# The weight parts of a two-layer encoder kernel begin a few bytes off a 64-byte multiple, at another place in each stage

## The chip, the cores and the metric

The kernel is one program on one core of a Trainium2 chip. The metric is the device time of one execution in microseconds. Before the change it is 1512.05 us, the median of two runs (1512.05 and 1512.06).

The engines are named as the profile names them: PE is TensorE's matmul stream and PEld its weight loads, DVE is VectorE, ACT is ScalarE, POOL is GpSimd, SP is the engine that issues most transfers. A matmul of this kernel loads a 128 x 128 weight (the *loaded* operand) and then streams up to 512 columns of another tile through it (the *streamed* operand).

## The reference

The reference is a two-layer trunk over a sequence of 512 positions with 1,024 features, with a memory of 256 positions, all in float32:

```python
for layer in range(DEPTH):
    xn = rms_norm(x, mix_norm[layer])
    if layer % 2 == 0:
        mixed = fox_diff_mixer(xn, ...)      # forgetting + differential attention
    else:
        mixed = mlstm_mixer(xn, ...)         # chunkwise mLSTM
    x = x + mixed
    x = x + memory_cross_attention(rms_norm(x, ...), rms_norm(mem, ...), wq, wkv, wo)
    x = x + conv_ffn(rms_norm(x, ...), w_up, conv_w, conv_b, w_down)
return rms_norm(x, final_norm)
```

Each layer thus has three stages: a mixer, a cross-attention over the memory and a gated FFN with a depthwise convolution (hidden width 2 x 2816). Nearly all arithmetic is in products of activations with weights.

## The kernel before, in words

**Split products.** A float32 product is formed from parts. Each weight block arrives by DMA in a tile `raw` (128 x 1024 floats). ScalarE writes its rounded high part to a tile `wh` (`split`, L262, or L1159 in the FFN), VectorE subtracts and writes the rest to a tile `wl` (`sub`, L259). Both have the type fp32r. Activations are kept as two parts as well, `xh` and `xl`. `mm3` (L268 to L270) then issues three matmuls for one 128 x 128 block: wh with xh, wh with xl, wl with xh, all three into one PSUM bank. The weight part is the loaded operand there, the activation is streamed. In `p_proj_tok` (L329 to L331) it is the other way round: the activations are loaded and the weight parts are streamed; this makes the values of the attentions and of the mLSTM. In `p_gate` (L542, L543) the weight of a few gate columns, 40 in the first mixer and 100 in the second, is loaded from a `wh` tile in which eight such blocks lie one behind the other.

**The tiles.** `raw`, `wh` and `wl` come from one pool with three buffers each. Every tile of this size in the program begins at a multiple of 64 bytes within its partition (small paddings, `pad`, see to that for some). So every 128-column weight block, 512 bytes, begins on such a multiple too. I call a multiple of 64 a *line* below. Of the larger tiles only the second buffer of `hs`, the rows that the convolution reads, begins 32 bytes off one; the convolution's taps (L1254) read `hs` from element 0, 1 or 2 on, and its second half begins 514 elements in.

**Stages and order.** A planner (`Plan`) sets the order for mixers and cross-attentions, a list scheduler (`Sched`) for the FFNs, both in Python with their own cost figures while the program is written; each engine then works its list in order. Parts of the next cross-attention's memory projections are made within the mixer.

**The FFN.** The up projection of a pair of 128-column blocks is done in one of two ways: plainly with 512-column matmuls, or, for nine of 22 pairs a layer (`SEVEN`), by seven products of half size with 256-column matmuls (`seven`). Of these seven, four load from `wh` and `wl` tiles (X first, th into `s`, X second, th into `acc`, of 12 matmuls each); the others load from tiles of their own, `s2`, `s4` and `a22`. `th` and `tl` are prepared activations. Between the products lie `fill` steps, pieces of the down projection with 512-column matmuls (rows `w<-ah,wh`). The memory projections of the cross-attentions (rows `acc<-mem,wh` of 256 columns) and the last projections of the program (`acc<-ah,wh` of 256 columns) are the other 256-column work on `wh`.

Of the kernel before, what the change touches and what calls it, by code (L numbers as in the profile page):

```python
# [9 lines left out]
F32 = mybir.dt.float32  # L10
F32R = mybir.dt.float32r
# [5 lines left out]
P = 128  # L17
# [34 lines left out]
class Item:  # L52
    def __init__(self, fn, dur, deps, prio, take, free, chain, pre, after, order, load, st):
        self.fn, self.dur, self.deps, self.prio, self.st = fn, dur, list(deps), prio, st
        self.take, self.free, self.chain, self.pre, self.after = take, free, chain, pre, after
        self.order, self.load = [o for o in order if o is not None], load
        self.ready = None


class Plan:  # L60
# [11 lines left out]
    def add(self, fn, dur=0.0, deps=(), prio=None, take=(), free=(), chain=(), pre=(), after=0.0, order=(), load=(), st=None):  # L72
        it = Item(fn, dur, [d for d in deps if d is not None], len(self.items) if prio is None else prio, take, free, chain, pre, after, order, load, st)
        it.n = len(self.items)
        self.items.append(it)
        return it
# [138 lines left out]
        self.now, self.idle = now, idle  # L215


class Builder:
    def __init__(self, tc, t):
        self.tc, self.nc, self.t = tc, tc.nc, t  # L220
# [26 lines left out]


    def weight_tiles(self):
        return [self.til(self.wp, tag, (P, 1024), dtype, bufs=3) for tag, dtype in (("raw", F32), ("wh", F32R), ("wl", F32R))]  # L250

    def weight(self, src, cols=1024):
        raw, hi, lo = self.weight_tiles()
# [264 lines left out]
    def gate_weights(self, src, m, parts):  # L518

        nc = self.nc  # L520
        raw = self.til(self.sp, "gw", (P, 8, m), bufs=1)
        nc.scalar.dma_start(raw[:], src)
        both = self.til(self.wp, "wh", (P, 1024), F32R, bufs=3)[:, : 8 * parts[-1][2]].rearrange("p (a b) -> p a b", a=8)
        nc.vector.memset(both.bitcast(F32), 0.0)
        for a, hi, lo, n in [(p[0], p[1], p[2] - p[3], p[3]) for p in parts]:
            h = both[:, :, hi : hi + n]
            nc.vector.tensor_copy(h, raw[:, :, a : a + n])
            self.sub(both[:, :, lo : lo + n], raw[:, :, a : a + n], h)
        return both
# [589 lines left out]
    def ffn_steps(self, layer, mp):  # L1119
# [3 lines left out]
        nc, t = self.nc, self.t  # L1123
# [23 lines left out]
            return add("SP", 0.0017 * cols, fn, (), at, [(tag, st)], (), 2.0)  # L1147

        def parts(st):
            st["wh"], st["wl"] = (self.til(self.wp, n, (P, 1024), F32R, bufs=3) for n in ("wh", "wl"))  # L1150

        def weight(src, cols, at, tag="raw"):

            st = {}
            l = load(st, tag, src, cols, at - 9.0)

            def hi():
                parts(st)
                nc.scalar.copy(st["wh"][:, :cols], st[tag][:, :cols])  # L1159

            h = add("ACT", act(cols), hi, [l], at - 3.0, [("h", st)])
            lo = add("DVE", tt(cols), lambda: self.sub(st["wl"][:, :cols], st[tag][:, :cols], st["wh"][:, :cols]), [h], at - 2.0, (), [(tag, st)])
            return st, lo
# [137 lines left out]
        def seven(p, fill):  # L1301
# [24 lines left out]
            def sum4(out, a, b):  # L1326
                if not sums.get("t"):
                    sums["t"] = self.til(mp, "sum", (P, 1536), bufs=1)
                tt_(out=out(), in0=a(), in1=b(), op=ALU.add)

            w3 = split(f3, 1024, [l2], at, lambda: parts(f3), [("h", f3)], lambda: r2["raw"][:])
            b1 = add("DVE", tt(512), lambda: sum4(S1, A21, A22), [l1], at - 6.0, [("sum", sums)])
            b2 = add("DVE", tt(512), lambda: sum4(S2, S1, A11), [b1, l2], at - 5.5)
            b3 = add("DVE", tt(512), lambda: sum4(S3, A21, A11), [b1, l2], at - 5.0)
            w2 = split(s2, 512, [b2], at, lambda: small(s2, "s2"), [("s2", s2)], S2)
            b4 = add("DVE", tt(512), lambda: sum4(S4, S2, A12), [w2], at - 1.5)
            w1 = split(f1, 1024, [b3], at + 1.0, lambda: parts(f1), [("h", f1)], lambda: sums["t"][:, :1024])
            w22 = split(a22, 512, [l1], at + 4.0, lambda: small(a22, "a22"), [("a22", a22)], A22)
            w4 = split(s4, 512, [b4], at + 5.0, lambda: small(s4, "s4"), [("s4", s4)], S4)
# [95 lines left out]
        if layer == 0:  # L1435
            for m in range(8):
                e = down(4, m, 2)
                a = add("ACT", 1.43, lambda m=m: self.xprep(m, "mix", 1, state), [e], clock[0] + 3.0)
# [261 lines left out]
    def run(self):  # L1700
        tc = self.tc
        M = bass.MemoryType.PSUM
        with (
            tc.tile_pool(name="cp", bufs=1) as self.cp,
            tc.tile_pool(name="xp", bufs=1) as self.xp,
            tc.tile_pool(name="sp", bufs=1) as self.sp,
            tc.tile_pool(name="wp", bufs=1) as self.wp,
            tc.tile_pool(name="acc", bufs=1, space=M) as self.acc,
            tc.tile_pool(name="aux", bufs=1, space=M) as self.aux,
        ):  # L1710
            self.constants()
            self.pad(self.cp, 32)
            self.pad(self.sp, 64)
            for layer in range(2):
                with tc.tile_pool(name=f"mem{layer}", bufs=1, reuse_waits="tile") as self.memp:
                    (self.mix0, self.mix1)[layer]()
                    self.xattn(layer)
                self.ffn(layer)


# [86 lines left out]
```

## Time and profile before

| | |
|---|---|
| median of the runs | 1512.05 us |
| the profiled execution | 1512.78 us |
| its span, first to last instruction | 1511.0 us |
| granted TensorE clock, mean over the span | 0.998 |
| PE busy, matmuls | 1500.0 us, 8026 |
| PEld busy, loads | 1281.7 us, 8026 |
| DVE busy | 1160.1 us |
| ACT busy | 774.8 us |
| POOL busy | 44.0 us |
| read from HBM | 143.04 MB |

The profiled execution is one run of the program; the span leaves out what lies before its first and behind its last instruction. A row of the groups gives line, engine, operation, out<-in tiles, shape and count, then busy time and mean of one in ns, then the engine's idle time in front. Matmuls overlap in the records: a mean of 390 ns doesn't say how far apart they start. The timeline gives each instruction's start and duration in us. The view of one line gives min/median/max in ns.

The stages follow each other like this: first mixer to about 262 us, cross-attention to 405, FFN to 768; second mixer to about 1015, cross-attention to 1166, FFN to the end.

### The profile page before, as it was taken

To read this page: it belongs to the slowest core of one execution; us is meant where nothing else is said; L and a number is where in the kernel's file an instruction comes from. 1 tells how busy PE (TensorE), PEld (TensorE's weight loads), DVE (VectorE), ACT (ScalarE), POOL (GpSimd) and SP (SyncE) were. 2 spreads that over 40 slices of the span, in tenths; PEclk is the share of its full clock that TensorE was granted. 3 is DMA by queue.
4 is the path that set the end of the run, shared out by engine and by line. 5 is a ranking of instruction groups with operands and counts; after the bars stand their busy time and mean duration, and the time that the engine had idled before them with its cause. 6 is when DMAs were issued, how large, how long until landed. Compare 5 with 4: busy or idle time off the path is not lost.

```text
span 1511.0 us, 21313 instructions
## 1 busy us (share of the span) xinstructions
PE 1500.0 (99%) x8026; PEld 1281.7 (85%) x8026; DVE 1160.1 (77%) x2155; ACT 774.8 (51%) x1282; POOL 44.0 (3%) x118
## 2 busy tenths in 40 slices
PE   9999999999999999999999999999999999999998
PEld 8888888888888888988888778888888888888887
DVE  7889885766699788897678857666557988889864
ACT  6768564444465444454446634444445554444444
POOL 2000120000000000000001100000000000000000
PEclk9999999999999999999999999999999999999999
DMA  5222233323223333232222222332323332333322
GB/s 179 84 71 84 84 103 108 112 96 100 95 101 100 97 108 109 84 112 88 81 90 84 80 89 93 99 101 99 111 84 109 108 94 95 98 103 106 102 60 77
DMA packets 47480, 146.52 MB, mean 97 GB/s; under 512 B 5649, under 2 KB 5649, under 8 KB 47377
## 3 DMA queue, kind: packets, MB, share of 16 engines
q1 hardware_dynamic: 46368, 144.04, 29.4%
q8 instruction: 63, 1.03, 0.3%
q10 hardware_dynamic: 1008, 1.12, 0.2%
q14 instruction: 41, 0.33, 0.1%
HBM read 143.04 MB, written 2.10 MB: 96 GB/s over the span
## 4 chain that ended last, share of the span: by engine, by line
PE 92%; DVE 3%; ACT 2%; issue 1%; DMA 1%; POOL 0%; SPq 0%; DVEq 0%; POOLq 0%; ACTq 0%
PE acc L268 19%; PE acc L269 19%; PE acc L270 19%; PE w L269 5%; PE w L268 5%; PE w L270 5%; PE acc L330 2%; PE acc L331 2%; PE acc L329 2%; PE s L268 2%; PE s L269 2%; PE s L270 2%; PE w L1595 1%; PE w L681 1%; PE s L395 1%
## 5 line engine op out<-in xcount | busy, mean ns | idle before, releaser
L268 PE MATMUL acc<-xh,wh 128*128 128x512 f32 (+1 forms) x944 | 356.9, 378 | 0.0
L270 PE MATMUL acc<-xh,wl 128*128 128x512 f32 (+1 forms) x944 | 352.8, 374 | 0.0
L269 PE MATMUL acc<-xl,wh 128*128 128x512 f32 (+1 forms) x944 | 352.6, 374 | 0.0
L259 DVE TENSOR_TENSOR wl<-raw,wh 128x1024 fp32r<-128x1024 f32 (+2 forms) x215 | 258.0, 1200 | 51.9 <-ACT wh L262 38.1
L262 ACT CAST wh<-raw 128x1024 fp32r<-128x1024 f32 (+2 forms) x137 | 140.9, 1030 | 168.5 <-PE acc L269 99.6
L270 PEld LDWEIGHTS acc<-xh,wl 128*128 128x128 f32 x944 | 177.5, 188 | 31.7
L268 PEld LDWEIGHTS acc<-xh,wh 128*128 128x128 f32 x944 | 177.6, 188 | 30.4
L269 PEld LDWEIGHTS acc<-xl,wh 128*128 128x128 f32 x944 | 177.7, 188 | 30.3
L1254 DVE SCALAR_TENSOR_TENSOR c<-hs,vec,c 128x512 f32<-128x512 f32 x176 | 128.4, 746 | 7.4 <-ACT c L1247 6.8
L269 PE MATMUL w<-al,wh 128*128 128x512 f32 x304 | 118.5, 390 | 0.0
L268 PE MATMUL w<-ah,wh 128*128 128x512 f32 x304 | 118.5, 390 | 0.0
L270 PE MATMUL w<-ah,wl 128*128 128x512 f32 x304 | 118.3, 389 | 0.0
L1159 ACT CAST wh<-raw 128x1024 fp32r<-128x1024 f32 (+1 forms) x60 | 61.3, 1022 | 77.8 <-PE acc L269 49.3
L1247 ACT ACTIVATE c<-hs,vec 128x512 f32<-128x512 f32 x88 | 70.0, 812 | 40.2 <-DVE hs L1393 23.5
L495 DVE TENSOR_TENSOR x<-w,x 128x512 f32<-128x512 f32 x72 | 49.5, 687 | 31.9 <-PE w L270 31.6
L270 PEld LDWEIGHTS w<-ah,wl 128*128 128x128 f32 x304 | 57.1, 188 | 12.0
L268 PEld LDWEIGHTS w<-ah,wh 128*128 128x128 f32 x304 | 57.1, 188 | 10.9
L269 PEld LDWEIGHTS w<-al,wh 128*128 128x128 f32 x304 | 57.1, 188 | 10.7
L1159 ACT CAST wh<-dr 128x512 fp32r<-128x512 f32 x64 | 39.7, 620 | 47.9 <-issue 17.4
L1268 ACT CAST ah<-c 128x512 fp32r<-128x512 f32 x44 | 27.3, 620 | 68.9 <-DVE c L1264 68.9
L330 PE MATMUL acc<-wl,xh 128*128 128x256 f32 (+1 forms) x192 | 61.9, 323 | 0.2 <-DVE wl L259 0.2
L329 PE MATMUL acc<-wh,xh 128*128 128x256 f32 (+1 forms) x192 | 61.7, 326 | 0.0
(373 smaller groups left out, 3323.4 us busy)
## 6 DMA issues: line engine op xcount, KB each, us to landing
raw<-in_up_dram SPq DMA_DIRECT2D x88, 512.0 KB, 3.3
dr<-in_down_dram SPq DMA_DIRECT2D x64, 256.0 KB, 2.6
raw<-in_xk_dram SPq DMA_DIRECT2D x16, 512.0 KB, 3.3
raw<-in_wo_dram SPq DMA_DIRECT2D x16, 512.0 KB, 3.2
raw<-in_xq_dram SPq DMA_DIRECT2D x16, 512.0 KB, 3.3
raw<-in_xv_dram SPq DMA_DIRECT2D x16, 512.0 KB, 3.3
raw<-in_xo_dram SPq DMA_DIRECT2D x16, 512.0 KB, 3.3
raw<-in_down_dram SPq DMA_DIRECT2D x16, 384.0 KB, 3.0
```

What stands on the lines that cost most here:

```text
L259: self.nc.vector.tensor_tensor(out=lo, in0=v, in1=hi.bitcast(F32), op=ALU.subtract)
L262: self.nc.scalar.copy(hi, v)
L268: mm(out, wh, xh, start=first, stop=False, skip_group_check=parts)
L269: mm(out, wh, xl, start=False, stop=False, skip_group_check=parts)
L270: mm(out, wl, xh, start=False, stop=last, skip_group_check=parts)
L329: mm(ps, xh[k][:, ts], wh[:, ws], start=(k == 0), stop=False)
L330: mm(ps, xh[k][:, ts], wl[:, ws], start=False, stop=False)
L331: mm(ps, xl[k][:, ts], wh[:, ws], start=False, stop=(k == 7))
L495: self.nc.vector.tensor_tensor(out=self.x[m][:], in0=ps[:], in1=self.x[m][:], op=ALU.add)
L1159: nc.scalar.copy(st["wh"][:, :cols], st[tag][:, :cols])
L1247: nc.scalar.activation(st["c_"][:, j, :], hs()[:, j, 2:514], AF.Identity, scale=self.col("cw", (layer * 3 + 2) * 44 + blk), bias=self.col( ...
L1254: nc.vector.scalar_tensor_tensor(out=c, in0=hs()[:, j, n : n + 512], scalar=w, in1=c, op0=ALU.mult, op1=ALU.add)
```

## The change

The tiles `wh` and `wl` get 1,088 columns in place of 1,024, and the parts are written to and read from columns `place` to `place + 1024`. `place` is set for each stage:

| | mixer | cross-attention | FFN |
|---|---|---|---|
| layer 0 | 2 (8 bytes) | 3 (12 bytes) | 1 (4 bytes) |
| layer 1 | 4 (16 bytes) | 60 (240, 16 below 256) | 63 (252, 4 below 256) |

`raw`, `dr` and the activations stay where they were in their tiles, and so do `s2`, `s4` and `a22`. The gates' weights, which share the tile `wh`, move too. The six tiles grow by 256 bytes each; to make room, the area for descriptors of dynamic DMAs at the start of the memory goes from 16,384 to 1,024 bytes. All other tiles thereby lie 13,824 to 15,360 bytes lower, by whole multiples of 512 outside the pool of `raw`, `wh` and `wl` and by multiples of 256 within it.

```diff
+PLACES = ((2, 3, 1), (4, 60, 63))
...
     def weight_tiles(self):
-        return [self.til(self.wp, tag, (P, 1024), dtype, bufs=3) for tag, dtype in (("raw", F32), ("wh", F32R), ("wl", F32R))]
+        return [self.til(self.wp, "raw", (P, 1024), bufs=3), self.part_tile("wh"), self.part_tile("wl")]
+
+    def part_tile(self, tag):
+
+        return self.til(self.wp, tag, (P, 1088), F32R, bufs=3)[:, self.place : self.place + 1024]
...
         nc.scalar.dma_start(raw[:], src)
-        both = self.til(self.wp, "wh", (P, 1024), F32R, bufs=3)[:, : 8 * parts[-1][2]].rearrange("p (a b) -> p a b", a=8)
+        both = self.part_tile("wh")[:, : 8 * parts[-1][2]].rearrange("p (a b) -> p a b", a=8)
...
         def parts(st):
-            st["wh"], st["wl"] = (self.til(self.wp, n, (P, 1024), F32R, bufs=3) for n in ("wh", "wl"))
+            st["wh"], st["wl"] = (self.part_tile(n) for n in ("wh", "wl"))
...
                 with tc.tile_pool(name=f"mem{layer}", bufs=1, reuse_waits="tile") as self.memp:
+                    self.place = PLACES[layer][0]
                     (self.mix0, self.mix1)[layer]()
+                    self.place = PLACES[layer][1]
                     self.xattn(layer)
+                self.place = PLACES[layer][2]
                 self.ffn(layer)
...
-    nc = _bacc.Bacc("TRN2", target_bir_lowering=False, num_devices=1)
+    nc = _bacc.Bacc("TRN2", target_bir_lowering=False, num_devices=1, dynamic_dma_scratch_size=1024)
```

## The prediction

> **What bounds the kernel now.** I read the page first: the busy times and the chain that ended last.
>
> ```profile
> span 1511.0 us, 21313 instructions
> PE 1500.0 (99%) x8026; PEld 1281.7 (85%) x8026; DVE 1160.1 (77%) x2155; ACT 774.8 (51%) x1282; POOL 44.0 (3%) x118
> ...
> PE 92%; DVE 3%; ACT 2%; issue 1%; DMA 1%; POOL 0%; SPq 0%; DVEq 0%; POOLq 0%; ACTq 0%
> ```
>
> TensorE is busy 99% of the span, and 92% of the chain is its own instructions one behind the other. Then the waits: first TensorE's view, whose weight row is the last below, then ScalarE's, whose longest wait stands in the second fence.
>
> ```profile
> PE acc L330 <- DVE wl L259: 0.2, 1, 0.2
> ```
>
> ```profile
> ACT wh L262 <- PE acc L269: 99.6, 40, 4.4
> ```
>
> TensorE waited for a weight's low part once, for 0.2 us. ScalarE, which makes the high part, waited 99.6 us for TensorE to release a buffer. So the parts are ready early, and neither engine that makes them sets the end. What counts is the time from one matmul's start to the next. Busy means (390 ns and so on) overlap and don't show it; the timeline of TensorE does. First, how many matmuls read a changed tile (by line and form; each L268 row has twins of the same count in L269 and L270):
>
> ```profile
> L268 PE MATMUL acc<-xh,wh 128*128 128x512 f32 x800 | 316.4, 395 | 0.0
> L268 PE MATMUL w<-ah,wh 128*128 128x512 f32 x304 | 118.5, 390 | 0.0
> L268 PE MATMUL acc<-mixed,wh 128*128 128x512 f32 x104 | 40.9, 393 | 0.1
> L268 PE MATMUL acc<-xh,wh 128*128 128x256 f32 x144 | 40.5, 281 | 0.0
> L268 PE MATMUL acc<-mem,wh 128*128 128x256 f32 x128 | 36.6, 286 | 0.0
> L329 PE MATMUL acc<-wh,xh 128*128 128x256 f32 x128 | 36.5, 293 | 0.0
> L268 PE MATMUL acc<-mem,wh 128*128 128x512 f32 x64 | 24.9, 389 | 0.0
> L268 PE MATMUL acc<-th,wh 128*128 128x256 f32 x72 | 20.2, 280 | 0.0
> L268 PE MATMUL s<-th,wh 128*128 128x256 f32 x72 | 19.9, 276 | 0.0
> L268 PE MATMUL acc<-mh,wh 128*128 128x512 f32 x48 | 19.0, 395 | 0.0
> L268 PE MATMUL acc<-ah,wh 128*128 128x256 f32 x36 | 10.3, 285 | 0.0
> ```
>
> With the changed tile as the loaded weight there are (800+304+104+64+48) x 3 = 3,960 matmuls of 512 columns, and (144+128+72+72+36) x 3 = 1,356 of 256. In L329 to L331 the weight is the streamed operand instead: the row of 128 above, times 3, and as many again of 512 columns.
>
> Now the pace, in the timeline of one block of the first FFN (rows between left out; columns: start, duration):
>
> ```profile
> 687.28 0.28 PE L268 MATMUL acc<-xh,wh 128*128 128x256 f32 x1
> ...
> 688.71 0.29 PE L268 MATMUL acc<-th,s2h 128*128 128x256 f32 x1
> ...
> 690.09 0.28 PE L268 MATMUL s<-th,wh 128*128 128x256 f32 x1
> ...
> 691.45 0.28 PE L268 MATMUL acc<-xh,wh 128*128 128x256 f32 x1
> ...
> 692.87 0.40 PE L268 MATMUL w<-ah,wh 128*128 128x512 f32 x1
> ...
> 693.34 0.39 PE L270 MATMUL w<-ah,wl 128*128 128x512 f32 x1
> ...
> 694.26 0.39 PE L268 MATMUL w<-ah,wh 128*128 128x512 f32 x1
> ...
> 695.62 0.28 PE L268 MATMUL acc<-th,wh 128*128 128x256 f32 x1
> ...
> 697.03 0.39 PE L268 MATMUL w<-ah,wh 128*128 128x512 f32 x1
> ...
> 699.75 0.28 PE L268 MATMUL acc<-th,a22h 128*128 128x256 f32 x1
> ```
>
> Each product has 12 matmuls. Divide: X with wh (687.28 to 688.71) 119.2 ns a matmul; th into s (690.09 to 691.45) 113.3; X again (691.45 to 692.87) 118.3; th into acc (695.62 to 697.03) 117.5. For 512 columns, 697.03 to 699.75 gives 226.7, exactly twice 113.3, but the stretch behind a switch from 256 columns starts slower: two matmuls in 0.47 us (235), six in 1.39 us (231.7), before it settles. So **the pace settles into one of a few steps**, with 113.3 and 226.7 the best seen, and 118 to 120 a common worse one at 256 columns. The memory projections sit in the worse one, 24 matmuls in 2.87 us, 119.6 each:
>
> ```profile
> 309.18 0.28 PE L268 MATMUL acc<-mem,wh 128*128 128x256 f32 x1
> ...
> 312.05 0.29 PE L268 MATMUL s<-kth,qh 128*128 128x256 f32 x1
> ```
>
> **The change part by part.** The instructions are the same, in the same order on every engine with the same waits (the built programs compared); only addresses move. So nothing is issued, queued or awaited anew, and no DMA changes its size. Three things can have a price.
>
> *The descriptor area shrinks to 1,024 bytes.* Queues of the profile:
>
> ```profile
> q1 hardware_dynamic: 46368, 144.04, 29.4%
> q8 instruction: 63, 1.03, 0.3%
> q10 hardware_dynamic: 1008, 1.12, 0.2%
> q14 instruction: 41, 0.33, 0.1%
> ```
>
> All data goes over the two hardware queues; no other queue is named that would use the area. Cost 0. All other tiles move by whole multiples of 256 bytes, so they keep their place within a 64-byte line; cost 0.
>
> *ScalarE writes wh, VectorE reads wh and writes wl off the line.* The trace of before has such accesses: the conv rows `hs` are read and written 8 bytes or more off a line, by a tap at n=1 4 bytes off, and by a tap at n=0 and j=0 on the line or 32 off. The rows with min/median/max:
>
> ```profile
> L1254 DVE SCALAR_TENSOR_TENSOR c<-hs,vec,c x176: 740/746/753, 433.0 to 1458.1; 128x512 f32<-128x512 f32 x176
> ```
>
> ```profile
> L1291 DVE TENSOR_TENSOR hs<-acc,rb x52: 680/686/692, 430.7 to 1455.7; 128x512 f32<-128x512 f32 x52
> ```
>
> ```profile
> L259 DVE TENSOR_TENSOR wl<-dr,wh x64: 678/683/693, 467.8 to 1459.9; 128x512 fp32r<-128x512 f32 x64
> ```
>
> ```profile
> L1220 ACT ACTIVATE hs<-x,vec x16: 705/710/717, 417.2 to 1175.2; 128x512 f32<-128x512 f32 x16
> ```
>
> The 176 taps with three kinds of start lie within 13 ns. Off-line writes by VectorE take 686 ns against 683 on the line, and ScalarE's writes (half of the 16 on a line or 32 off, half 8 bytes off those) lie within 12 ns. So I take 0; at most 13 ns a part, covered by ScalarE's 99.6 us of waiting. Without that cover it would be some 300 parts x 13 ns = 4 us.
>
> *TensorE loads and streams the weights off the line.* This is the term. The load itself, and the only off-line loads of before, the gates' (L542, L543; the groups by line, the view of line 542 with min/median/max, and the timeline):
>
> ```profile
> L268 PEld LDWEIGHTS w<-ah,wh 128*128 128x128 f32 x304 | 57.1, 188 | 10.9
> ```
>
> ```profile
> L542 PEld LDWEIGHTS w<-xh,wh x16: 114/141/164, 7.2 to 770.9; 128*40 128x40 f32 x8, 128*100 128x100 f32 x8
> ```
>
> ```profile
> 767.89 0.39 PE L542 MATMUL w<-xh,wh 128*100 128x512 f32 x1
> ...
> 771.56 0.40 PE L329 MATMUL acc<-wh,xh 128*128 128x512 f32 x1
> ```
>
> The second gate's eight weights of 100 columns lie 400 bytes apart, so six of them begin 16, 32 or 48 bytes off a line. Their loads take at most 164 ns, those of 40 columns at least 114: 50 ns for 60 columns, by which 128 columns would take 187, and the loads on the line do take 188. So the load itself shows no price for such a start. The matmuls do: 16 in 3.67 us, 229.4 ns each, 2.7 over the settled 226.7. No row shows a load that begins 4, 8 or 12 bytes off, and none a streamed operand off its line.
>
> Bounds. **Below:** every matmul on a changed tile settles at 113.3 or 226.7. X first: 18 blocks x 12 x 5.9 ns = 1.3 us; X second, 216 x 5.0 = 1.1; th into acc, 216 x 4.2 = 0.9; memory, 384 x 6.3 = 2.4; the last projections (ah, 256), 108 x 6.3 = 0.7 if at the memory's pace. That is 6.4 us. Behind a switch to 512 columns 6 x 5.0 = 30 ns are lost; about three switches in each of 18 blocks make 1.6 us. Together 8.0 us; the streamed 256-column work could add 384 x 6.3 = 2.4 us, which I keep for the range. **Above:** every load at the gate's price: 2.7 ns x (3,960 + 1,356) = 14.4 us; for the streamed weights I have no row and take the same 2.7 ns x 768 = 2.1 us; together 16.5 us. The farther end is the worst pace seen in the transitions, 235, held: 8.3 x 3,960 = 33 us.
>
> Which? Two of the products above read th and wh and take 113.3 and 117.5; all four tiles begin on a line, so a small difference in how streaming and loading meet decides between steps. A shift of the load by a few elements changes just this meeting, and four of the five stretches of 256 columns above stand in a bad step, from which a move mostly leads down; the 512-column work is already settled and has 226.7 - 188 = 39 ns of room for a longer load. Nearest to these rows is the lower end, and I take half of it: **-4.0 us**. Sum: span 1511.0 - 4.0 = 1507.0; the profiled execution took 1512.78 us, 1.8 outside the span, so 1508.8; it stood 0.7 above the median of 1512.05, so **1508.1 us**.
>
> [...]
>
> **The rivals.** *(a) Each load gets longer.* If it is read in pieces as large as the change's largest shift, 16 bytes, a weight row of 512 bytes begun off a piece takes 33 for 32, and a 32nd of the load's 188 ns is 5.9 ns. At 512 columns the 39 ns of room hide it; at 256 the load fills the pace and all of it shows: 1,356 x 5.9 = 8.0 us, to 1520; with 2.7 ns on the long ones as in the gate, 1531. It speaks for this that the gate's matmuls never settled; against it, that they are only 16, fewer than one settled product plus its transition. It decides against me as soon as the extra exceeds the 3 ns a matmul which my 4.0 us over 1,356 amount to. *(b) The 512-column work loses its settled pace* and holds the 235 of the transition: +33 us, 1545, slower by over 2%. For: 235 occurs. Against: it lasts for two matmuls. The point is 30.2 / 3,960 = 7.6 ns a matmul. *(c) Nothing happens:* the pace settles by itself wherever the load starts; 1512, within 1 us. For: 226.7 holds with `ah`, `mixed` and `xh` alike. *(d) The settled 226.7 is itself a collision of load and stream* that the shift removes. One more step down, as large as that from 235 to 226.7, is 8.3 x 3,960 = 33 us: 1479, faster by over 2%. Against it: 226.7 is twice 113.3, so this time follows the columns, not the loads, and no stretch shows less.
>
> **How the numbers follow.** My forecast, 1501 to 1511: 0.50. (c) 0.14. (a) 0.22. (b), with any larger price on long or streamed matmuls: 0.10. (d) 0.04. The range 1501 to 1530 leaves out (b), (d) and the last of (a), under 0.2. 2% is 30.2 us, about what a measurement of this kernel can tell from no change: faster than 1481.8 only in (d), 0.04; slower than 1542.3 in (b), 0.10; within, 0.86.
>
> **What the profile after would show.** The same counts; ScalarE and VectorE groups within 13 ns; 512-column stretches at 226.7 away from switches (else b); X, th and memory products nearer 113.3 (else a or c); the load's mean still 188 (a longer one is a). I would be wrong if a stage with odd starts, 4 or 12 bytes, paces differently from those at 16 bytes, or if L329 to L331 stream the shifted weights slower, which nothing here bounds from a row of its own.

## The result, and the profile after

The changed kernel takes 1531.15 us (1531.07 and 1531.24) against 1512.05: ratio 1.0123, 95% interval 1.0103 to 1.0143. It is 19.1 us slower, where I had forecast 4 us less and a range that ended at 1530.

The page of the changed kernel, in the parts that I showed of before. Its line numbers are those of before plus 8, so L268 to L270 are L276 to L278, and L329 to L331 are L337 to L339.

```profile
span 1529.5 us, 21313 instructions
PE 1518.0 (99%) x8026; PEld 1281.6 (84%) x8026; DVE 1161.1 (76%) x2155; ACT 775.0 (51%) x1282; POOL 43.3 (3%) x118
...
PE 91%; DVE 4%; ACT 3%; issue 1%; DMA 1%; POOL 0%; SPq 0%; DVEq 0%; POOLq 0%; ACTq 0%
```

The same instructions, and TensorE still is the chain. Its busy time grew by 18.0 us, the span by 18.5; the others stand still (DVE +1.0, ACT +0.2). The loads' busy time did not grow at all (1281.7 to 1281.6). TensorE's waits for a weight part, and ScalarE's longest wait for a buffer, by the chain of waits of each engine:

```profile
PE acc L338 <- DVE wl L267: 0.4, 1, 0.4
PE acc L337 <- ACT wh L270: 0.4, 1, 0.4
```

```profile
ACT wh L270 <- PE acc L277: 101.9, 42, 4.5
```

0.8 us of waits against 0.2: the parts still come early. So the 18.5 us are TensorE's own pace. The groups of matmuls by line and form:

```profile
L276 PE MATMUL acc<-xh,wh 128*128 128x512 f32 x800 | 319.2, 399 | 0.0
...
L276 PE MATMUL w<-ah,wh 128*128 128x512 f32 x304 | 119.8, 394 | 0.0
...
L276 PE MATMUL acc<-mem,wh 128*128 128x256 f32 x128 | 36.3, 284 | 0.0
...
L337 PE MATMUL acc<-wh,mem 128*128 128x512 f32 x64 | 25.2, 393 | 0.0
...
L276 PE MATMUL acc<-mem,wh 128*128 128x512 f32 x64 | 24.9, 389 | 0.0
```

The first two long rows rose by 4 ns (395 to 399, 390 to 394), the memory's short one fell by 2 (286 to 284), and its long one stood still (389). The row of the streamed weights, L337, rose by 4 (389 to 393). A mean is no pace, but it follows it: in the stretch of TensorE alone further below, 48 matmuls at 226.7 ns each have records of 389 ns in the mean, and 48 at 233.4 have 395.5. The pace itself, in the timeline of the same block of the first FFN as before (start, duration), then one stretch of the memory's projections and one of the second FFN:

```profile
311.10 0.28 PE L276 MATMUL acc<-mem,wh 128*128 128x256 f32 x1
...
313.90 0.28 PE L276 MATMUL s<-kth,qh 128*128 128x256 f32 x1
...
693.84 0.28 PE L276 MATMUL acc<-xh,wh 128*128 128x256 f32 x1
...
695.25 0.29 PE L276 MATMUL acc<-th,s2h 128*128 128x256 f32 x1
...
696.64 0.28 PE L276 MATMUL s<-th,wh 128*128 128x256 f32 x1
...
698.06 0.28 PE L276 MATMUL acc<-xh,wh 128*128 128x256 f32 x1
...
699.48 0.39 PE L276 MATMUL w<-ah,wh 128*128 128x512 f32 x1
...
702.27 0.28 PE L276 MATMUL acc<-th,wh 128*128 128x256 f32 x1
...
703.69 0.39 PE L276 MATMUL w<-ah,wh 128*128 128x512 f32 x1
...
706.48 0.28 PE L276 MATMUL acc<-th,a22h 128*128 128x256 f32 x1
...
1301.55 0.40 PE L276 MATMUL w<-ah,wh 128*128 128x512 f32 x1
...
1304.35 0.28 PE L276 MATMUL acc<-th,wh 128*128 128x256 f32 x1
```

| product | matmuls | before, ns each | after, ns each |
|---|---|---|---|
| memory, 256 columns | 24 | 119.6 | 116.7 |
| X first | 12 | 119.2 | 117.5 |
| th into s | 12 | 113.3 | 118.3 |
| X second | 12 | 118.3 | 118.3 |
| th into acc | 12 | 117.5 | 118.3 |
| ah, 512 columns, second stretch | 12 | 226.7 | 232.5 |
| ah, 512 columns, second FFN | 12 | | 233.3 |

In these stretches two short products improved as forecast, two got worse, one stayed. What decides is the 512-column row: it does not come back to 226.7 behind a switch. Where this happens is seen from the same three matmuls in both timelines, at the ends of the first FFN and the start of the second; first before, then after:

```profile
405.18 0.39 PE L270 MATMUL acc<-mem,wl 128*128 128x512 f32 x1
...
768.11 0.39 PE L543 MATMUL w<-xl,wh 128*100 128x512 f32 x1
...
1166.00 0.39 PE L268 MATMUL acc<-xh,wh 128*128 128x512 f32 x1
```

```profile
407.01 0.39 PE L278 MATMUL acc<-mem,wl 128*128 128x512 f32 x1
...
776.46 0.39 PE L551 MATMUL w<-xl,wh 128*100 128x512 f32 x1
...
1177.12 0.40 PE L276 MATMUL acc<-xh,wh 128*128 128x512 f32 x1
```

The first FFN took 362.9 us and takes 369.5 (+6.5), the second, to the end of the span, 345.0 and 352.4 (+7.4). That is 14 of the 18.5 us. The mixers and cross-attentions together gave the other 4.6. Added up over every start in the timeline, the 4,170 matmuls of 512 columns that load a part in `mm3` cost 15.7 us more, those that stream one 1.6, and the 256-column ones that load one 1.1.

### The profile page after: what moved, and what is told of

Read it like the earlier page. It is cut to its first block, busy times and chain, and to the rows that moved or that the text cites. A ratio compares the mean times of both kernels' runs of the same rounds, so it can differ in the third digit from the quotient of the medians.

```text
span 1529.5 us, 21313 instructions
## 1 busy us (share of the span) xinstructions
PE 1518.0 (99%) x8026; PEld 1281.6 (84%) x8026; DVE 1161.1 (76%) x2155; ACT 775.0 (51%) x1282; POOL 43.3 (3%) x118
## 4 chain that ended last, share of the span: by engine, by line
PE 91%; DVE 4%; ACT 3%; issue 1%; DMA 1%; POOL 0%; SPq 0%; DVEq 0%; POOLq 0%; ACTq 0%
PE acc L276 19%; PE acc L277 19%; PE acc L278 19%; PE w L277 5%; PE w L278 5%; PE w L276 5%; PE acc L338 2%; PE acc L339 2%; PE acc L337 2%; PE s L276 2%; PE s L278 2%; PE s L277 2%; PE w L1603 1%; PE w L689 1%; DVE wl L267 1%
## 5 line engine op out<-in xcount | busy, mean ns | idle before, releaser
L276 PE MATMUL acc<-xh,wh 128*128 128x512 f32 (+1 forms) x944 | 359.7, 381 | 0.0
L278 PE MATMUL acc<-xh,wl 128*128 128x512 f32 (+1 forms) x944 | 355.3, 376 | 0.0
L270 ACT CAST wh<-raw 128x1024 fp32r<-128x1024 f32 (+2 forms) x137 | 140.8, 1028 | 172.2 <-PE acc L277 101.9
L278 PEld LDWEIGHTS acc<-xh,wl 128*128 128x128 f32 x944 | 177.7, 188 | 34.7
L276 PEld LDWEIGHTS acc<-xh,wh 128*128 128x128 f32 x944 | 177.4, 188 | 33.4
L278 PE MATMUL w<-ah,wl 128*128 128x512 f32 x304 | 119.8, 394 | 0.0
L276 PE MATMUL w<-ah,wh 128*128 128x512 f32 x304 | 119.8, 394 | 0.0
L278 PEld LDWEIGHTS w<-ah,wl 128*128 128x128 f32 x304 | 57.0, 188 | 13.6
L1167 ACT CAST wh<-dr 128x512 fp32r<-128x512 f32 x64 | 39.7, 620 | 56.3 <-PE acc L277 19.1
L276 PEld LDWEIGHTS w<-ah,wh 128*128 128x128 f32 x304 | 57.1, 188 | 12.4
L339 PE MATMUL acc<-wh,xl 128*128 128x256 f32 (+1 forms) x192 | 61.8, 323 | 0.0
L337 PE MATMUL acc<-wh,xh 128*128 128x256 f32 (+1 forms) x192 | 61.3, 325 | 0.4 <-ACT wh L270 0.4
```

The source lines that it names most:

```text
L270: self.nc.scalar.copy(hi, v)
L276: mm(out, wh, xh, start=first, stop=False, skip_group_check=parts)
L278: mm(out, wl, xh, start=False, stop=last, skip_group_check=parts)
L337: mm(ps, xh[k][:, ts], wh[:, ws], start=(k == 0), stop=False)
L339: mm(ps, xl[k][:, ts], wh[:, ws], start=False, stop=(k == 7))
```

## The experiments

A *start* below is how many elements of 4 bytes a part begins behind the start of its tile. All kernels but the changed one are compared with the kernel before on the same chip in the same session; there it stood at 1512.67 to 1513.18. Three numbers of a `PLACES` pair are mixer, cross-attention and FFN of a layer. Where no ratio is given, a kernel ran once; single runs of the kernel before lay between 1512.0 and 1514.3, so there I read stages and paces rather than a difference of a us or two. Paces by stage that have no fence are means over the starts in the timeline, with the long gaps at switches and waits left out. The line numbers of `mm3` move by one or more where an edit adds lines.

My first theory behind the result was that a weight row that leaves its 64-byte line costs the stream; the rival was that something else of the edit (the wider tiles, the smaller descriptor area) does.

**All parts at 0, the rest of the change kept.**

```diff
-PLACES = ((2, 3, 1), (4, 60, 63))
+PLACES = ((0, 0, 0), (0, 0, 0))
```

> All six places are 0; the wider tiles and the small descriptor area stay. Theory 1 (the place alone costs): 1512 us within 1, the FFNs' 512-column stretches back at 226.7 ns a matmul. Rival (the moved tiles or the small area cost): it stays near 1531.

1512.72 us, ratio 1.0001 (0.9991 to 1.0010). The second FFN's row, in the groups between 1200 and 1500 us:

```profile
L276 PE MATMUL w<-ah,wh 128*128 128x512 f32 x128 | 49.9, 390 | 0.0
```

Tile width, pool layout and descriptor area cost nothing. The start alone costs the 19 us.

**The starts exchanged between the layers.**

```diff
+PLACES = ((4, 60, 63), (2, 3, 1))
```

> The places of the two layers are exchanged: first FFN at 63, second at 1. Theory 1 (the pace goes with the place): the first FFN's 512-column stretches take 233 ns a matmul and the second's 232, and the whole 1530 to 1533 us. Rival (the pace goes with the stage): 232 in the first and 233 in the second as after the change.

1530.58 us. The pace went with the start, not with the layer: the first FFN at 63 took 232.9 ns a 512-column matmul, the second at 1 took 232.3 (in the changed kernel 233.2 at 63 and 232.1 at 1). Streamed parts did the same: 233.3 at 60 and 229.0 at 3, in whichever layer.

**Larger shifts: whole lines, and both ends of the change's range.**

```diff
+PLACES = ((16, 16, 4), (32, 32, 60))
```

> FFNs at 4 and 60 (16 bytes behind and ahead of a multiple of 64), the other stages of layer 0 at 16 (64 bytes) and of layer 1 at 32 (128 bytes). Theory 1, that only a start off a multiple of 64 costs: the mixers and cross-attentions are back within 0.5 ns of before at 512 columns. Theory 1a, that the cost falls as the shift grows to whole 16-byte pieces: the FFNs stand between 227 and 231 ns a matmul, total 1514 to 1522 us. Rival (any shift in this size costs alike): 232 to 233 in the FFNs, total 1525 us.

```diff
+PLACES = ((8, 8, 8), (16, 16, 16))
```

> All of layer 0 at 8 (32 bytes), all of layer 1 at 16 (64 bytes). Theory 1: layer 1 is back at the pace of before, 226.7 ns in the FFN, 256 columns apart; layer 0 at 32 bytes pays, some 230 to 233 ns. Total 1518 to 1524 us. Rival (phase against the streamed operand within 128 bytes decides): layer 1 differs from before, its 256-column products nearer 113 or 120 and the total below 1512 or above 1524.

1530.90 and 1536.42 us. The groups of the first FFN (420 to 760 us) and of the second (1200 to 1500 us), of the first of the two kernels (starts 4 and 60), then of the second (8 and 16):

```profile
L276 PE MATMUL w<-ah,wh 128*128 128x512 f32 x149 | 58.6, 393 | 0.0
...
L276 PE MATMUL w<-ah,wh 128*128 128x512 f32 x128 | 50.0, 391 | 0.0
```

```profile
L276 PE MATMUL w<-ah,wh 128*128 128x512 f32 x147 | 58.0, 395 | 0.0
...
L276 PE MATMUL w<-ah,wh 128*128 128x512 f32 x128 | 50.6, 395 | 0.0
```

A start at 16, which is 64 bytes and on a line, costs in full: 395, or 233.2 to 233.3 ns in the timeline, in all three stages of the layer. So does 8. But 60, off the line, costs least: 391, or 228.2 ns. The theory of the line falls. The second kernel, whose starts are whole multiples of 32 and 64 bytes, is the slowest of all.

The next theory was that of a *meeting*: the distance between where the load begins and where the stream begins decides, with a period of 256 bytes. In the kernel before, every part and every streamed `xh`, `ah` and `mem` begins at the same place modulo 256 bytes. `th` and `tl` begin elsewhere, 192 bytes further on by that count, and the best short pace, 113.3 ns, was one of theirs: equal places were not what it needed.

**The streamed tiles moved in both FFNs, the loaded ones in the first alone.**

```diff
+PLACES = ((0, 0, 63), (0, 0, 0))
+STREAM = 63
-                acts[p] = tuple(self.til(mp, n, dtype=F32R, bufs=10) for n in ("ah", "al"))
+                acts[p] = tuple(self.til(mp, n, (P, 576), F32R, bufs=10)[:, STREAM : STREAM + 512] for n in ("ah", "al"))
```

> In both feed-forward stages the streamed parts ah and al begin 63 elements (252 bytes) into wider tiles; the weights' parts begin at 63 in layer 0's feed-forward stage and at 0 everywhere else; xh and xl stay where they were. Theory of the meeting (the pace goes with the distance between the loaded operand's start and the streamed operand's start): in layer 0's stage the products that stream ah and al have distance 0 and settle at 226.7 to 227 ns a 512-column matmul, while those that stream xh and xl stay at 232 to 233; in layer 1's stage it is the reverse, ah and al at 231 to 233, xh and xl at 227. Theory of the place alone (the loaded operand's own start decides): all 512-column products of layer 0's stage at 232 to 233, all of layer 1's at 227. By both the time lies near 1519 us (some 6 to 7 us over before), so the rows decide, not the time.

1517.01 us. Both theories failed in part. The groups of the first FFN (420 to 760 us), then of the second (1200 to 1500 us):

```profile
L278 PE MATMUL acc<-xl,wh 128*128 128x512 f32 x204 | 80.2, 393 | 0.0
...
L277 PE MATMUL w<-ah,wh 128*128 128x512 f32 x158 | 61.7, 391 | 0.0
...
L277 PE MATMUL acc<-xh,wh 128*128 128x512 f32 x144 | 56.1, 390 | 0.0
...
L277 PE MATMUL w<-ah,wh 128*128 128x512 f32 x128 | 49.8, 389 | 0.0
```

In the second FFN the streamed tile stood 252 bytes on, 4 short of the period, and nothing was lost (227.2 ns), against the meeting. In the first FFN the same loaded start that had cost 233 with the streamed tiles at 0 now cost 229.2 for `ah` and 230.6 for `xh`, against a rule of the loaded start alone.

**One part of the two moved.** The first FFN has `wh` at 63 and `wl` at 0, the second the reverse.

```diff
+PLACES = ((0, 0, "wh"), (0, 0, "wl"))
-        return self.til(self.wp, tag, (P, 1088), F32R, bufs=3)[:, self.place : self.place + 1024]
+        at = 63 if tag == self.place else 0
+        return self.til(self.wp, tag, (P, 1088), F32R, bufs=3)[:, at : at + 1024]
```

> Layer 0's feed-forward stage has only the high parts (wh) at 63, layer 1's only the low parts (wl); all else begins at 0. If each load pays for its own place: layer 0's stage gains two thirds of what it gained when both parts were off (6.5 us, so 4.3: near 367 us in place of 363), layer 1's a third (7.3, so 2.4: near 347.5 in place of 345.0), and the time is near 1519 us. If one load out of place unsettles the whole run of matmuls that follow it: both stages pay in full, 369 and 352 us, time near 1526 us.

1516.41 us; the stages took 364.0 and 346.8 us. `wh`, two of three loads, cost 1.1 us alone; `wl`, one of three, 1.8. Neither share of the sum of loads nor the whole price, so neither expectation held. The second FFN's groups (1200 to 1500 us):

```profile
L277 PE MATMUL w<-ah,wh 128*128 128x512 f32 x128 | 50.3, 393 | 0.0
L278 PE MATMUL w<-al,wh 128*128 128x512 f32 x128 | 50.2, 392 | 0.0
L279 PE MATMUL w<-ah,wl 128*128 128x512 f32 x128 | 49.6, 388 | 0.0
```

With one load of three moved, all three matmuls changed, one of them downward. The row of that one before, in the same window:

```profile
L270 PE MATMUL w<-ah,wl 128*128 128x512 f32 x128 | 49.8, 389 | 0.0
```

From start to start the step shows more: the three took 227.6, 227.9 and 226.8 ns before and take 230.4, 231.4 and 224.9; the one that loads the moved part is the one that got shorter. In the timeline most groups of three take 686 or 687 ns together, where three of 226.7 take 680: one step of 6.7 ns more for the three. So no load pays for itself. The three run as one rhythm.

**Shifts of 256, 192 and 128 bytes.**

```diff
+PLACES = ((64, 64, 32), (48, 48, 64))
```

> Starts at 256 bytes (layer 0's mixer and cross-attention, layer 1's feed-forward stage), at 192 bytes (layer 1's mixer and cross-attention) and at 128 bytes (layer 0's feed-forward stage). Theory of the meeting with a period of 256 bytes: the stages at 256 bytes go at before's pace (261, 143 and 345 us; 227 to 228 ns a 512-column matmul), those at 192 and 128 bytes at 231 to 233 ns (layer 1's mixer near 249.5, layer 0's feed-forward near 370 us); time near 1524 us. If any start other than the tile's own costs: all stages at 233 ns, near 1536 us. If the period is 128 bytes: layer 0's feed-forward stage also back at 363 us, near 1517 us.

1521.33 us. The groups of the first FFN, at 128 bytes (420 to 760 us), and of the second, at 256 bytes (1200 to 1500 us):

```profile
L276 PE MATMUL w<-ah,wh 128*128 128x512 f32 x155 | 61.1, 394 | 0.0
...
L276 PE MATMUL w<-ah,wh 128*128 128x512 f32 x128 | 49.9, 390 | 0.0
```

At 256 bytes the cross-attention and the second FFN went as before (143.0 and 345.0 us), and so did the pace in all three stages: 228.4, 227.5 and 227.1 ns for the 512-column matmuls that load a part, against 228.3, 227.4 and 227.1. The first mixer took 262.5 us from its first matmul, against 261.2; the difference lies in waits within its first 45 us, as it does with one part moved, where the first mixer stood at 0 and was as long. At 128 bytes these matmuls took 232.2 ns, at 192 about 229. So a shift of 256 bytes is free, in line with a period of 256; no other two starts that lie 256 bytes apart were tried.

**Only the 256-column weights moved**, to keep what the change gained. The X tile of the FFNs and the weights of the memory's projections begin off their tile, all else at 0. The core of the edit:

```diff
+PLACES = ((0, 0, 0), (0, 0, 0))
+NARROW_X, NARROW_MEM = (16, 48), (16, 2)
-            w3 = split(f3, 1024, [l2], at, lambda: parts(f3), [("h", f3)], lambda: r2["raw"][:])
+            w3 = split(f3, 1024, [l2], at, lambda: parts(f3, NARROW_X[layer]), [("h", f3)], lambda: r2["raw"][:])
```

> All 512-column products keep their weights at 0; only weights that are used with 256-column streams are moved: the X tile of the feed-forward stages to 16 (layer 0) and 48 (layer 1), the memory projection's to 16 and 2. Theory of the meeting: 512-column pace stays 227 in every stage, the 256-column products of these weights go from 119 to 120 ns down to 115 to 118, some 2 to 4 ns on several hundred matmuls: 1 to 3 us less than before, 1509 to 1511 us. If the gain of the 256-column products only came with the slower 512-column pace around them: no change, 1512 us.

1512.69 us, ratio 0.9999 (0.9989 to 1.0008). The 512-column pace stayed, and the memory's products fell from 119.2 to 114.6 ns in the first mixer and from 119.8 to 116.2 in the second; but all these products are only some 380 matmuls, worth 1.2 us, and the second FFN took 0.7 us more. There th into `s`, whose own tiles had not moved, went from 113.3 to 117.8 ns; in the first FFN, where the X tile stood at 16 and not at 48, it stayed at 113.3. The gain is too small to measure.

**TensorE alone.** Behind the last output of the kernel with all starts at 0 I put some 3,000 matmuls with nothing beside them: tiles of zeros written once, the pattern of `mm3`, 48 matmuls for each case behind 24 that set the entry. It adds work and changes no output.

```diff
+        for first, runs in PROBES:
+            for name, ph, pl, at in runs:
+                steps("from" + "pq"[first > 0], first, first)
+                steps(name, ph, pl, 2, at=at)
```

`first` is 0 (`fromp`) or 16 (`fromq`), `ph` and `pl` are the starts of the high and low part, `at` that of the streamed tile.

> The kernel with all parts at 0, and behind its last output a stretch of matmuls alone: tiles written once with zeros, then on TensorE, with no work of VectorE or ScalarE beside it, 48 matmuls of 512 columns at each of 14 starts of both loaded parts (0 to 63 elements), each behind 24 at start 0 and again, in a second pass, behind 24 at start 16; then only the high part or only the low part off, then the streamed tile off. Outputs unchanged; some 2,600 matmuls more, time near 2150 us. Theory of the loaded operand's place: with TensorE alone the pace repeats that of the kernel by place: 226.7 ns at 0, 228 to 229 at 3 and 60, 231 to 232 at 1 and 2, 233 at 4, 8, 16 and 63; the streamed tile's place changes nothing by itself (226.7 at 1, 16 and 63). Rival (the other engines' writes into off-line tiles hold TensorE): every start at 226.7 ns here. Second pass: by a pace that depends on the place alone the same values; if the matmuls lock into one of several paces by how they are entered, some starts (above all 4, 60 and 63) differ between the passes by 3 to 7 ns.

First, the busy time of each engine in that stretch; it shows that no other engine works:

```profile
core 0: us, PE busy (x) PEld busy (x) DVE busy (x) ACT busy (x) POOL busy (x), PEclk, DMA share, GB/s
1530.00:2160.00 630.00, 630.00 (x2906) 520.96 (x2904) 0.00 (x0) 0.00 (x0) 0.00 (x0) 1.00 0.00 1
```

Then its timeline. `ond` and `red` are the same case, both parts at 3, entered from the two sides; `loa` has only the low part at 1; `xa` has the loads at 0 and the streamed tile at 1:

```profile
1575.58 0.39 PE L285 MATMUL ond<-px,wh 128*128 128x512 f32 x1
...
1586.46 0.39 PE L285 MATMUL fromp<-px,wh 128*128 128x512 f32 x1
...
1790.07 0.39 PE L285 MATMUL loa<-px,wh 128*128 128x512 f32 x1
...
1801.25 0.40 PE L285 MATMUL fromp<-px,wh 128*128 128x512 f32 x1
...
1823.05 0.40 PE L285 MATMUL xa<-px,wh 128*128 128x512 f32 x1
...
1834.41 0.39 PE L285 MATMUL fromp<-px,wh 128*128 128x512 f32 x1
...
1939.17 0.39 PE L285 MATMUL red<-px,wh 128*128 128x512 f32 x1
...
1950.36 0.40 PE L285 MATMUL fromq<-px,wh 128*128 128x512 f32 x1
```

Each block is 48 matmuls: 10.88 us or 226.7 ns for `ond`, 11.18 or 232.9 for `loa`, 11.36 or 236.7 for `xa`, 11.19 or 233.1 for `red`. All cases, settled, from the same timeline:

| both parts at | behind start 0, ns | behind start 16, ns |
|---|---|---|
| 0 | 226.7 | 226.7 |
| 1 | 232.3 | 232.5 |
| 2 | 230.7 | 230.5 |
| 3 | 226.7 | 233.3 |
| 4 | 226.7 | 233.3 |
| 8 | 233.4 | 233.4 |
| 16 | 233.4 | 233.4 |
| 24 | 234.3 | 234.5 |
| 32 | 232.2 | 232.7 |
| 48 | 229.0 | 233.3 |
| 56 | 233.3 | 233.3 |
| 60 | 226.7 | 226.7 |
| 62 | 233.3 | 233.3 |
| 63 | 226.7 | 233.3 |

Only the high part off: 231.1 at 1, 226.7 at 63. Only the low: 233.3 at 1, 226.7 at 63. The streamed tile off, loads at 0: 236.7 at 1, 228.9 at 16, 226.7 at 63. All of them at 63: 228.3. With 256 columns: 120.0 at 0, 118.3 at 4, 117.8 at 16, 120.0 at 63.

The rival falls: the price is there with no other engine at work. The theory of the loaded start falls as a rule by itself, since a streamed tile 4 bytes off, with the loads at 0, costs the most of all; that of the meeting too, since equal places at 63 don't give the pace of equal places at 0. And four starts (3, 4, 48, 63) have two paces, each of which holds for all 48 matmuls: the matmuls lock into one by how they are entered. The two passes also write to other pairs of the kernel's four PSUM banks `acc0` to `acc3`, but the bank alone doesn't sort them: start 63 was fast in banks 0 and 3 and slow in 1 and 2, start 3 the other way round. Starts 0 and 60 come back to 226.7 from either side.

**Does the table carry to the kernel?** All parts at 3, then all at 60, two of the starts off a line that showed 226.7 in it. At 3 the pace depended on what ran before, at 60 it did not.

```diff
+PLACES = ((3, 3, 3), (3, 3, 3))
```

> All stages begin their parts at 3 elements (12 bytes), where the cross-attention of the changed kernel settled at 6 steps of 6.67 ns for three matmuls, as before the change does. Theory of the loaded operand's place: feed-forward stages near 227 to 228 ns a matmul (363 to 365 and 345 to 347 us), mixers 228 to 230, the time 1512 to 1518 us, most of the changed kernel's loss gone with the parts still off. If every start off the tile's own costs alike in the feed-forward stages: 232 to 233 ns there, and 1528 to 1531 us.

```diff
+PLACES = ((60, 60, 60), (60, 60, 60))
```

> All stages begin their parts at 60 elements (240 bytes), the only start beside the tile's own that went back to 226.7 ns from both entries in the stretch of matmuls alone. If that decides in the kernel too: 512-column matmuls at 227 to 228.5 ns in every stage (the feed-forward stage that stood at 60 earlier had 228.2), stages near 262, 143.5, 365, 247.5, 151 and 347 us, time 1514 to 1518 us. If the kernel's order of work (switches between products, 256-column runs, two streamed parts) throws it into the slow pace as it did at 3 elements: 230 ns and more in the mixers, 1520 us or more.

At 3: 1521.22 us, ratio 1.0053 (1.0036 to 1.0070), above what I gave. The mixers went at 232.1 ns, the cross-attentions at 228.9 and 228.0, the FFNs at 229.6 and 229.3. With one start in all stages, the matmuls that stream `mixed` took 227.1 and 227.0 ns in the cross-attentions and 233.3 in the second mixer: the two paces of the table, in the kernel. (Three matmuls at 226.7 ns take 680 ns, 102 steps of 6.67 ns; the 6 steps in the expectation are not a count of the whole.)

At 60: 1519.40 us, ratio 1.0040 (1.0026 to 1.0055), again above, by 1.4 us. Here the matmuls that load a part went nearly as I expected (228.3, 227.6, 228.2, 228.2, 227.4 and 228.2 ns by stage), and so did the stages (262.1, 143.7, 365.3, 247.9, 151.4, 346.9 us). My range did not fit my own stages: they add up to 1516.0, and with 1.0 us ahead of the first matmul and 1.8 outside the span to 1518.8. What I had not looked at are the parts as streamed tiles, which cost some 2.6 us here; the 512-column matmuls that load a part cost some 3.4. In the groups by line and form:

```profile
L337 PE MATMUL acc<-wh,mem 128*128 128x512 f32 x64 | 25.4, 398 | 0.0
```

398 against 389 before: 234.6 ns at this start in the first cross-attention, while as loaded tiles the same parts have a good place. One start need not suit both uses.

**Only the FFNs back at 0.**

```diff
+PLACES = ((2, 3, 0), (4, 60, 0))
```

> Mixers and cross-attention as in the changed kernel (starts 2, 3, 4, 60), the two feed-forward stages back at 0. If the loss sits where the stage lengths say, 6.5 and 7.3 us go: near 1517 us. If the feed-forward stages only show a loss that is made ahead of them, 1525 us or more.

1518.43 us: 12.7 less than the changed kernel, where the stage lengths promised 13.9, and with the FFNs at 363.0 and 345.0 us as before. So the FFNs' loss hangs on their own starts, not on what runs ahead of them.

No version beat the kernel before. By the time of the whole kernel, a start at 0 for loaded and streamed tiles is the best in these runs.

## Why the prediction was wrong, point by point

**What held.** TensorE bounds, the parts are early, and the descriptor area and the other tiles' move cost nothing (1.0001 with all else kept). The other engines' accesses cost next to nothing, in the view of one line each:

```profile
L1262 DVE SCALAR_TENSOR_TENSOR c<-hs,vec,c x176: 741/747/754, 435.0 to 1475.6; 128x512 f32<-128x512 f32 x176
```

```profile
L267 DVE TENSOR_TENSOR wl<-dr,wh x64: 681/685/695, 470.6 to 1477.5; 128x512 fp32r<-128x512 f32 x64
```

746 and 747, 683 and 685 ns at the median. The load is as long as before, too:

```profile
L276 PEld LDWEIGHTS acc<-xh,wh x944: 186/188/192, 28.4 to 1472.1; 128*128 128x128 f32 x189
```

So rival (a), the longer load, is out.

The pieces of 16 bytes that (a) reckons with are a supposition: no run shows them, and whether a start is a whole multiple of 16 bytes does not sort the costs. In TensorE's stretch alone 8, 16 and 32 elements, which are, cost 5.5 to 6.7 ns a matmul, and 3 and 63, which are not, can be free (226.7 ns).

**The step that failed** is the paragraph "Which?": "the 512-column work is already settled and has 226.7 - 188 = 39 ns of room for a longer load". Both halves of the sentence are true and neither bears on the case. The load did not get longer; the room behind it grew to 233.3 - 188 = 45 ns. What grew is the time from one matmul's start to the next, from 226.7 to as much as 233.3 ns, and that is 15.7 of the 18.5 us. And "settled" was a property of one start: I read from the transitions that the pace moves in steps, saw that a shift changes which step a product takes, applied this to the 1,356 short matmuls, most of which stood in a bad step, and not to the 3,960 long ones that stood in a good one. From a good step a move mostly led up: of the 13 other starts in the table of TensorE alone only 60 kept 226.7 from both sides, and none went below it. The count alone should have decided: three quarters of the matmuls had only something to lose. The rows held a second warning. The two products of `th` and `wh` at 113.3 and 117.5 ns begin at the same places modulo 256 bytes, so nothing in their starts told them apart; I read their difference as a sign of how load and stream meet.

**The sizes.** The gain of the short products came in the mixers and cross-attentions (119.2 to 116.7 ns and the like), some 0.6 us; in the FFNs they lost 1.7 us. I had put -4.0 on them and on the switches. The long loaded ones, put at 0, cost +15.7: some 4 ns each. They are 4,170 and not 3,960, since my count left out the smaller rows (`ah`, `v`, `ka`, `qa` and `q`). The streamed weights, which "nothing here bounds", cost 1.6, under the 2.1 that I had for them in the upper end. That end, 16.5 us, was the gate's price of 2.7 ns on everything; the measured price is 4 ns on three quarters of it. The gate was the nearest row and I gave it too little weight: it was the only one with loads off a line. That it never settled was too strong, though. Its eight blocks begin at eight places, and the gaps between its starts run from 226 to 237 ns, six in a row of them at 226 or 227.

**The rivals.** (b), the lost pace, is what happened, at 232 to 233 ns and mostly in the FFNs rather than at 235 everywhere, so 1531 and not 1545; its ground against itself ("it lasts for two matmuls") described the start of before, not the shifted one. (c) assumed that the pace settles by itself wherever the load starts; among 14 starts it does so at two, 0 and 60. (d) asked whether 226.7 already holds a collision; no 512-column stretch of a run went below it in the mean, so that stays open.

**What would have shown it:** of the marks that I named, three spoke: the 512-column stretches were not at 226.7 away from switches, stages paced differently by their start (228.5 ns at 12 bytes, 232.1 at 4, both in layer 0), and L337 to L339 streamed the shifted weights slower (229.0 and 233.3 ns in the cross-attentions, 226.7 before).

## What to carry to other kernels

When most of the work stands in its best observed state and a change moves what that state depends on, price the loss of the state over that work before the gain on the rest. Where split matmuls like these run back to back, look at the starts in the timeline, not at busy shares, to see whether the pace holds at the new place; of the shifts here, only the one by 256 bytes was free for loaded and streamed weights alike (the cross-attention, which has both, took 143.0 us as before, the second FFN 345.0). A cost per instruction was the wrong model for these matmuls: moving one load of three changed all three (227.6, 227.9 and 226.8 ns to 230.4, 231.4 and 224.9), and one place had two paces (226.7 and 233.3 ns).

## What the runs showed that I had not expected

Many of the paces stand on a grid. 113.3, 120.0, 226.7 and 233.3 ns are 17, 18, 34 and 35 steps of 6.67 ns, and three matmuls in a row sum to 102 steps at start 0, 103 at 48 behind start 0, 104 with only the high part at 1, 105 at 8 and 16. Starts 1, 2, 24 and 32 have no such whole number over three. In the changed kernel the settled 512-column matmuls lost up to one step each.

Two paces can be stable at one and the same place. With the parts at 3, 4 or 63 elements, 48 matmuls held 226.7 ns behind a good stretch and 233.3 behind a bad one, with equal places of loaded and streamed tiles and nothing else at work; at start 0 the bad one did not last: the 48 matmuls there behind start 16 settle at 226.7, with records of 389 to 390 ns in the mean against 389 behind start 0.

A streamed tile 4 bytes off, with the loads at 0, gave 236.7 ns, more than any shift of the loads; 4 bytes to the other side (63 elements, 252 bytes) gave 226.7. What in the memory or in TensorE makes the step, and why these two sides differ, no run here tells.

In TensorE's stretch alone, moving nothing but the loaded tiles' start from 0 to 16 slowed the matmul from 226.7 to 233.4 ns, with loads of 188 ns in the mean at either (`fromp` and `fromq`). So the pace of these matmuls depends on where the loads begin, though the load's own record gets no longer.
